# One encoder layer on one core: the MLP's up projection as seven products of halves, in turns with those of the down projection

## The chip, the cores and the metric

The kernel runs on one core of a Trainium2 chip. The metric is device time in microseconds (us) for one execution, weights read from HBM and outputs written back, everything between included. Less is better.

## What is computed

Two groups of 256 tokens share all weights, so the kernel treats them as T = 512 tokens of width D = 1024. In float32:

```
def encoder_layer(x, mem, ...):
    h = rms_norm(x, norm1_g)
    proj = h @ w_in                      # q, k, v of three attentions, three gates
    ... banded, dilated and memory attention ...
    merged = (sigmoid(ga) * (oa @ w_branch_a) + sigmoid(gb) * (ob @ w_branch_b)
              + sigmoid(gm) * (om @ w_branch_m))
    x = x + merged @ w_out
    h2 = rms_norm(x, norm2_g)
    x = x + jnp.square(jax.nn.relu(h2 @ w_up)) @ w_down    # w_up 1024 x 4096, w_down 4096 x 1024
    return x                             # then a final rms_norm
```

The change lies in the last three lines of the layer. The norm factor of h2 is not applied before the MLP: since the squared ReLU is homogeneous, the kernel multiplies the result of the down projection by the inverse mean square of each token (`rr`).

## The kernel before

**Three products for one.** Every float32 matrix is split into a rounded upper part (`hi`) and the remainder (`lo`), and `mm3` (line 193) makes one product as three TensorE matmuls: hi with hi, hi with lo, lo with hi. ScalarE (ACT) makes each hi by a copy, VectorE (DVE; in the attention stage GpSimd, POOL) makes each lo by a subtraction. A weight tile is 128 partitions by 1024 elements, 512 KB: one DMA, one ACT copy, one DVE subtraction.

**Units.** The program is a list of units, each a function and the weight tiles that it wants; `run()` calls them in order. Before the matmuls of a unit it fetches the tiles that are needed, behind them those of the next three needs (`ahead`): DMA, hi and lo stand that far ahead of their use. DVE, ACT and TensorE (PE) keep the order in which the program is written; the DMA queues of SyncE (SP) and POOL get theirs from a scheduler. Work on a finished product waits in a list, `later`, that is emptied (`flush`) behind the matmuls of the next unit. Subtractions for lo tiles wait in a list, `lows`, that `lower()` empties ahead of every unit.

**The stages.** Memory keys and values, the projections and attentions, the gates and branches, the output projection (`out_proj`, eight units of 24 matmuls, with h2 as eight tiles `h` of 128 features by 512 tokens), then the MLP.

**The MLP.** The 4096 inner features go in eight chunks `c` of 512. In chunk c, `up` makes four tiles of 128 features by 512 tokens, each in two halves of 12 matmuls of 512 columns; `put_up` takes ReLU and square on ACT into `UP`. The down projection of chunk c-1 stands between these halves, as seven products of halves instead of eight (Strassen's scheme in Winograd's form): `form` makes the sums of quarters of UP (DVE), their hi (ACT) and lo (DVE); `parts` makes the sums of quarters of the weights. One tile T holds a quarter, and becomes the next sum when POOL issues a DMA that adds another quarter onto it in place (`accum_op`), which has to wait for the lo tile that was made of it. `product` runs 12 matmuls of 512 columns, and `add_to` adds the two PSUM banks of a product to running sums (`acc`) on DVE. Chunk 7 is done without this (`last_down`): its weights and its four inner tiles (`LAST`) are used as they are, output quarter by output quarter.

Of the kernel before, what the change touches and what calls it, by code (L numbers as in the profile page):

```python
# [10 lines left out]
F32 = mybir.dt.float32  # L11
# [66 lines left out]
def encoder_kernel(ctx: ExitStack, tc: tile.TileContext, a: dict, out: bass.AP):  # L78
# [20 lines left out]
    def h2(s="h", dt=F32):  # L99
        return sb.tile([P, T], dt, tag="h2", name=nm(s), bufs=20)  # L100
# [10 lines left out]
    def f(x):  # L111
        return x.bitcast(F32)
# [57 lines left out]

    lows = []

    def lower(keep=0):
        for fn in lows[:len(lows) - keep]:
            fn()
        del lows[:len(lows) - keep]

    def run():
        need = [(i, s) for i, (_, srcs) in enumerate(units) for s in srcs]
        got, at = [[] for _ in units], 0  # L180
        done = 0
        for i, (fn, srcs) in enumerate(units):
            done += len(srcs)
            for fetch in (True, False):
                while at < min(len(need), done + (0 if fetch else ahead[0])):
                    u, s = need[at]
                    got[u].append(s[0]() if callable(s[0]) else chunk(*s))
                    at += 1
                if fetch:
                    lower()  # L190
                    fn(*got[i])

    def mm3(o, wh, wl, xh, xl, first, last, more=False):
# [565 lines left out]
        unit(flush)  # L759


    MG, wb, sg = [], [], {}

    def gate(w, ff, br):
# [40 lines left out]

    unit(lambda: merge(KD - 1))


    X1, H = [], []

    def out_proj(w):
        ff = len(H)
        r = h2("xr")
        A.dma_start(r, a["xT"][:, ff])
        p = bank()
        fm(w, M, p)
        V.tensor_tensor(r, p, r, op=ALU.add)
        X1.append(r)
        x = s4("h")
        A.activation(x[:, 0], r, AF.Copy, scale=gains[:, 2, ff:ff + 1])  # L820
        V.scalar_tensor_tensor(x[:, 1], r, gains[:, 2, ff:ff + 1], f(x[:, 0]), op0=ALU.mult,
                               op1=ALU.subtract)
        H.append(x)

    for ff in range(KD):
        unit(out_proj, (a["w_o"][ff],))

# [14 lines left out]
    def mlp_pool():  # L842
        stages.close()
        at[0] = stages.enter_context(tc.tile_pool(name="ml", bufs=1))

    def block_tile():
        return at[0].tile([P, 1024], F32, tag="blk", name=nm("blk"), bufs=8)

    def turn_x1(t, hh):

# [51 lines left out]
    def load_blocks(c):  # L902

        if c in blocks:
            return
        t = {n: block_tile() for n in "T2BC"}
        for n, b in (("T", "11"), ("2", "21"), ("C", "12"), ("B", "22")):
            SP.dma_start(t[n], block(c, b))
        G.dma_start(t["C"], block(c, "22"), accum_op=ALU.add)
        blocks[c] = t  # L910

    def parts(c, n):

        def go():
            load_blocks(c)
            hi, lo = w_tile(), w_tile()
            src = blocks[c][n[0]]
            A.activation(hi, src, AF.Copy)

            def low():  # L920
                V.tensor_tensor(lo, src, f(hi), op=ALU.subtract)
                if n[1:]:
                    G.dma_start(src, block(c, n[1:]), accum_op=ALU.add)  # L923

            lows.append(low)
            return hi, lo
        return go

# [2 lines left out]
    def form(c, name):  # L931

        lo, hi = UP[c, 0], UP[c, 1]
        A11, A21, A12, A22 = lo[:, :, :S], lo[:, :, S:], hi[:, :, :S], hi[:, :, S:]

        def less(u, v):
            d = h2("f").rearrange("p (j t) -> p j t", j=2)
            V.tensor_tensor(d, u, v, op=ALU.subtract)
            return d

        if name in ("P1", "P2", "Q4"):
            src = {"P1": A11, "P2": A12, "Q4": A22}[name]
        elif name == "Q5":
            src = forms[c, "S1"] = less(A21, A22)
        elif name == "Q6":
            src = forms[c, "S2"] = less(A11, forms.pop((c, "S1")))
        elif name == "P7":
            src = less(A11, A21)
        else:
            src = less(A12, forms.pop((c, "S2")))  # L950
        x = s4("f")
        xh, xl = (x[:, i].rearrange("p (j t) -> p j t", j=2) for i in range(2))
        A.activation(xh, src, AF.Copy)
        lows.append(lambda: V.tensor_tensor(xl, src, f(xh), op=ALU.subtract))
        forms[c, name] = x

    acc, banks = {}, {}

    def add_to(k, i, p, op=ALU.add):
        if (k, i) in acc:  # L960
            V.tensor_tensor(acc[k, i], acc[k, i], p, op=op)
        else:
# [1 line left out]
            A.activation(acc[k, i], p, AF.Copy, scale=1.0 if op == ALU.add else -1.0)  # L964


    PRODUCTS = dict(P1=("T12", "a", "V", -1), P2=("2", "a", "11", 1), Q5=("T22", "d", "G", 1),
                    Q6=("T21", "c", "V", 1), P7=("C", "e", "G", -1), Q3=("B", "d", "12", 1), Q4=("T", "e", "21", 1))

    def product(w, c, name):  # L970
        _, bk, to, sign = PRODUCTS[name]
# [86 lines left out]
    unit(mlp_pool)  # L1058
    ORDER = ("P1", "P2", "Q5", "Q6", "P7", "Q3", "Q4")


    SUMMED = {1: ("12", "12"), 2: ("11", "11"), 3: ("21", "21"), 4: ("12", "V"), 5: ("21", "V", 1), 6: ("22", "G")}

    def make(c, n):
        unit(lambda: form(c, ORDER[n]))

    for c in range(NC):
        for h in range(8):
            ff, half = 4 * c + h // 2, h % 2
            unit(lambda *w, ff=ff, half=half: up(w[0] if w else None, ff, half), *([(a["w_up"][ff],)] if half == 0 else []))  # L1070
            if c == 0:
                unit(lambda h=h: turn_x1(h % 4, h // 4))
            if h == 1 and c < NC - 1:
                unit(lambda c=c: load_blocks(c))
            if h == 7 and c == NC - 2:
                unit(fetch_x1)
            if c == NC - 1 and h == 6:
                unit(lambda: ahead.__setitem__(0, 2))
            if c == NC - 1 and h in SUMMED:
                unit(lambda n=SUMMED[h]: later.append(lambda: combine(*n)))  # L1080
            if c and h < 7:
                for n in ((1, 2) if h == 0 else (h + 2,)):
                    if n < 7:
                        make(c - 1, n)
                unit(lambda w, c=c - 1, n=ORDER[h]: product(w, c, n), (parts(c - 1, PRODUCTS[ORDER[h]][0]),))
        if c == 0:
            unit(inv_ms)
            unit(lambda: ahead.__setitem__(0, 3))
        if c < NC - 1:
            make(c, 0)  # L1090
    unit(lambda *w: (kept.update({(0, 0): w[0], (1, 0): w[1]}), last_down(0, (0, 1))),
         *[(block(NC - 1, n),) for n in ("11", "21")])
    unit(lambda: later.append(lambda: combine("22", "V")))
# [84 lines left out]
```

## Time and profile before

| | |
|---|---|
| median of 3 runs (lowest, highest) | 857.63 us (856.81, 858.55) |
| the profiled execution | 859.08 us |
| its span, from first to last instruction | 857.3 us |
| mean granted clock of PE | 0.993 |
| busy: PE, weight loads of PE, DVE, ACT, POOL | 844.4, 703.8, 462.8, 397.1, 216.0 us |

The profile is of one execution, 1.45 us above the median, with 1.8 us outside its span. A busy share is a mean over the whole span; what a change in one stage is worth has to be read in that stage. In the rows "ps" is a PSUM bank, "w" a hi or lo weight tile, "raw" and "blk" weight tiles as they come from HBM, "h" the tiles of h2, "f" a form, "u" inner features, "mg" the merged branches. Nearly every operation is recorded at L72, the line of a helper.

### The profile page before, as it was taken

The numbers are of one execution on the slowest core, as the hardware profiler recorded it, in microseconds if no ns is written. First come the engines' busy times: TensorE is split into PE (matmuls) and PEld (weight loads), VectorE is DVE, ScalarE is ACT, GpSimd is POOL, SyncE is SP. The second block draws the span as 40 slices with busy tenths as digits, with TensorE's granted clock in tenths as the row PEclk, the third lists the DMA queues.
The fourth block names the chain that finished last, engine by engine and source line by source line (L and its number), as shares of the span: only waits on it lengthen the run. The fifth ranks groups of instructions, "written<-read, shape, count | busy, mean of one in ns | idle before, by whom it ended". The sixth has DMA issues, their size and how long they took to land.

```text
span 857.3 us, 10785 instructions
## 1 busy us (share of the span) xinstructions
PE 844.4 (99%) x4080; PEld 703.8 (82%) x4080; DVE 462.8 (54%) x737; ACT 397.1 (46%) x690; POOL 216.0 (25%) x161
## 2 busy tenths in 40 slices
PE   9999999999999999999999999999999999999996
PEld 7788998888888888888888788888888888888885
DVE  6575535465452311423435542465767666767895
ACT  6455545565554333222323227564445353545453
POOL 2314554656556543211123000000000000000001
PEclk9999999999999999999999999999999999999998
DMA  8343122324241228432322445374747465645322
GB/s 284 115 119 109 62 99 86 98 63 115 85 119 64 75 74 286 132 99 86 110 99 74 147 147 161 110 204 107 205 109 208 111 185 121 178 120 172 75 75 98
DMA packets 47468, 106.87 MB, mean 125 GB/s; under 512 B 19358, under 2 KB 19604, under 8 KB 47416
## 3 DMA queue, kind: packets, MB, share of 16 engines
q1 hardware_dynamic: 39992, 85.69, 30.2%
q0 software_dynamic: 4256, 14.73, 9.7%
q10 hardware_dynamic: 3168, 5.77, 2.0%
q8 instruction: 32, 0.52, 0.3%
q14 instruction: 20, 0.16, 0.1%
HBM read 101.93 MB, written 4.24 MB: 124 GB/s over the span
## 4 chain that ended last, share of the span: by engine, by line
PE 84%; DVE 8%; ACT 5%; issue 2%; DMA 1%; POOL 0%; POOLq 0%; SPq 0%; DVEq 0%; ACTq 0%
PE ps L72 77%; PE sc L72 3%; PE o L72 2%; DVE w L72 2%; PE tp L72 2%; ACT w L72 2%; DVE f L72 1%; ACT sp L72 1%; DVE sp L72 1%; DMA mr<-in_memT 1%; ACT f L72 1%; DVE sq L72 0%; ACT r L72 0%; DVE mg L72 0%; DVE acc L72 0%
## 5 line engine op out<-in xcount | busy, mean ns | idle before, releaser
L72 PE MATMUL ps<-x,w 128*128 128x512 f32 x1080 | 252.5, 391 | 0.0
L72 PEld LDWEIGHTS ps<-x,w 128*128 128x128 f32 x1080 | 201.0, 188 | 41.3
L72 PE MATMUL ps<-h,w 128*128 128x512 f32 x768 | 184.5, 391 | 0.0
L72 PEld LDWEIGHTS ps<-h,w 128*128 128x128 f32 x768 | 143.7, 188 | 29.5
L72 PE MATMUL ps<-w,f 128*128 128x512 f32 (+1 forms) x696 | 164.1, 387 | 1.3 <-DVE acc L72 1.0
L72 DVE TENSOR_TENSOR w<-raw,w 128x1024 fp32r<-128x1024 f32 (+1 forms) x79 | 96.4, 1223 | 115.3 <-ACT w L72 115.2
L72 PEld LDWEIGHTS ps<-w,f 128*128 128x128 f32 x696 | 128.7, 188 | 29.9 <-issue 3.4
L72 ACT ACTIVATE w<-raw 128x1024 fp32r<-128x1024 f32 (+2 forms) x116 | 119.7, 1036 | 21.9 <-DMA raw<-in_w_mem 7.5
L161 POOL TENSOR_TENSOR w<-raw,w 128x1024 fp32r<-128x1024 f32 (+1 forms) x37 | 87.3, 2361 | 120.1 <-ACT w L72 94.9
L72 DVE TENSOR_TENSOR w<-blk,w 128x1024 fp32r<-128x1024 f32 x49 | 59.5, 1224 | 47.7 <-ACT w L72 47.6
L923 POOL DMA_DIRECT2D blk<-in_w_dn x21 | 18.1, 864 | 240.2 <-DVE w L72 240.2
L72 ACT ACTIVATE w<-blk 128x1024 fp32r<-128x1024 f32 x49 | 50.7, 1047 | 15.4 <-DMA blk<-in_w_dn 15.4
L72 DVE TENSOR_TENSOR acc<-acc,ps 128x512 f32<-128x512 f32 x82 | 52.9, 682 | 2.9 <-PE ps L72 2.9
L72 ACT ACTIVATE f<-f 128x512 fp32r<-128x512 f32 x28 | 17.7, 633 | 75.4 <-DVE f L72 75.4
L72 ACT ACTIVATE sp<-sp,st 128x256 f32<-128x256 f32 (+1 forms) x48 | 25.8, 538 | 57.7 <-DVE st L72 57.7
L72 ACT ACTIVATE g<-ps 128x512 f32<-128x512 f32 x16 | 9.6, 598 | 88.4 <-PE ps L72 88.4
L72 DVE TENSOR_TENSOR sum<-o,lo 64x256 f32<-64x256 f32 x24 | 10.0, 417 | 66.5 <-ACT lo L72 66.3
L72 PE MATMUL ps<-mg,w 128*128 128x512 f32 x192 | 44.2, 391 | 1.5 <-ACT mg L72 0.9
L72 PEld LDWEIGHTS ps<-mg,w 128*128 128x128 f32 x192 | 36.0, 188 | 9.6 <-ACT mg L72 1.3
L72 ACT ACTIVATE r<-ps 128x512 f32<-128x512 f32 x32 | 18.9, 591 | 50.7 <-PE ps L72 50.7
L72 PE MATMUL ps<-w,x 128*128 128x384 f32 (+1 forms) x192 | 39.9, 363 | 0.0
L469 POOL TENSOR_TENSOR sp<-sp,st 128x512 f32<-128x512 f32 (+1 forms) x32 | 36.7, 1147 | 6.5 <-DVE st L72 3.6
(146 smaller groups left out, 959.2 us busy)
## 6 DMA issues: line engine op xcount, KB each, us to landing
raw<-in_w_up SPq DMA_DIRECT2D x32, 512.0 KB, 4.7
blk<-in_w_dn SPq DMA_DIRECT2D x28, 512.0 KB, 6.7
blk<-in_w_dn POOLq DMA_DIRECT2D x28, 512.0 KB, 5.7
raw<-in_w_g SPq DMA_DIRECT2D x24, 512.0 KB, 3.3
raw<-in_w_b SPq DMA_DIRECT2D x12, 512.0 KB, 3.3
raw<-in_w_bam SPq DMA_DIRECT2D x8, 512.0 KB, 3.3
raw<-in_w_o SPq DMA_DIRECT2D x8, 512.0 KB, 3.2
raw<-in_w_mem SPq DMA_DIRECT2D x7, 512.0 KB, 3.3
```

Of the source, the lines that this page charges most:

```text
L72: return self.tc.keep_in_program_order(method(*args, **kw))
L161: sub[0].tensor_tensor(lo[:, c], raw[:, c], f(hi[:, c]), op=ALU.subtract)
L469: G.tensor_tensor(s[:, :, :w], s[:, :, :w], st[:, 6:8].unsqueeze(2).to_broadcast([P, 2, w]), op=ALU.mult)
L923: G.dma_start(src, block(c, n[1:]), accum_op=ALU.add)
```

## The change

1. **Up projection of chunks 1 to 7.** `seven` makes it of seven products. Rows of the result are halved by features (two tiles of 128 each), columns by group of tokens (256 each), the sum over 1024 by halves of 512. A product is 24 matmuls of 256 columns into one bank, 168 matmuls a chunk where there were 96 of 512 columns. Sums of quarters of the weights are made as in the down projection, with two tiles T and C and four accumulating DMAs a chunk; the quarters come from HBM in pieces of 2 KB. `take` puts the products together: three copies on ACT and five additions on DVE a chunk, and `put` takes ReLU and square.
2. **Sums of h2.** They are the same for all chunks, and `halves_of` makes them once, in eight steps, during chunk 0 (which keeps the plain `up`) and at the start of chunk 1. The last sum overwrites the second group's half of the first four h tiles.
3. **Turns.** One up product and one down product alternate, seven pairs a chunk. Both use the order P1, P2, Q5, Q3, Q6, P7, Q4, in which each sum held in T is used two pairs behind the one before; in the down projection Q6 stood right behind Q5. Quarters 21 and 22 are loaded by themselves into `raw` tiles rather than `blk` tiles.
4. **Lists.** `lower()` is gone. `tick()` stands at the head of `up`, of a product of either projection, and of `last_down` (there behind the flush). It runs what is in `wlows` (lo of weights, and the accumulating DMA that follows), in `lows` (lo of forms) and in `soon` (steps on ACT); what these add to the lists is run one tick later.
5. **Output projection.** The first two units are one: six eighths of the sum for both tiles first, then the last two eighths of each.
6. **Chunk 7.** Its inner tiles come by `put_last`, in pieces of 256 tokens.

```
+    def tick():
+        for todo in (wlows, lows, soon):
+            now = todo[:]
+            todo.clear()
+            for fn in now:
+                fn()
...
-                    lower()
...
+        def go(n, w):
+            tick()
...
+            for j in range(2):
+                for k in range(4):
...
+                    xh, xl = form_of(X, forms, n, k)
+                    mm3(b[:, j * S:(j + 1) * S], w[0][:, c], w[1][:, c], xh, xl, new and j == k == 0, k == 3, j > 0 or not new)
+            flush(9)
+            later.append(lambda: take(n, b))
...
-            lows.append(low)
+            wlows.append(low)
...
     def last_down(hh, ts, n0=0, n1=512, part=0):
         flush(9)
-        lower()
+        tick()
...
+    def put_last(i, h, r):
+        A.activation(r, r, AF.Square)
...
+        for j in range(2):
+            x, u, t = LAST[2 * h + j], r[:, j * S:(j + 1) * S], slice(i * S, (i + 1) * S)
+            A.activation(x[:, 0, t], u, AF.Copy)
+            lows.append(lambda x=x, u=u, t=t: V.tensor_tensor(x[:, 1, t], u, f(x[:, 0, t]), op=ALU.subtract))
```

The instructions move as follows at the three places of which the prediction speaks. On PE, at the start of the output projection before; mg711 and mg718 are the last two of the eight merged tiles, w698 and w699 hi and lo of the first weight tile:

```order
L72 MATMUL ps720_4077<-mg710_4021,w699_3969 128x512
L72 MATMUL ps720_4077<-mg711_4024,w698_3968 128x512 x2
L72 MATMUL ps720_4077<-mg711_4024,w699_3969 128x512
L72 MATMUL ps720_4077<-mg718_4072,w698_3968 128x512 x2
L72 MATMUL ps720_4077<-mg718_4072,w699_3969 128x512
L72 MATMUL ps726_4114<-mg705_4006,w703_4001 128x512 x2
```

and after, where the rows of the second weight tile (w703) with the first six merged tiles stand ahead of these:

```order
L72 MATMUL ps720_4080<-mg710_4021,w703_4001 128x512 x2
L72 MATMUL ps720_4080<-mg710_4021,w704_4002 128x512
L72 MATMUL ps719_4079<-mg711_4024,w698_3968 128x512 x2
L72 MATMUL ps719_4079<-mg711_4024,w699_3969 128x512
L72 MATMUL ps719_4079<-mg718_4072,w698_3968 128x512 x2
L72 MATMUL ps719_4079<-mg718_4072,w699_3969 128x512
```

The first use of mg718 was PE's 22nd matmul of the stage; it is now the 40th, behind 18 of each tile and three with mg711.

On DVE, after, one steady chunk has 44 instructions; these are those from the running sums of the first down product of a chunk (ps5962, ps5969) to those of the second:

```order
L72 TENSOR_TENSOR acc844_4744<-acc844_4744,ps1055_5962 128x512
L72 TENSOR_TENSOR acc845_4746<-acc845_4746,ps1056_5969 128x512
L72 TENSOR_TENSOR f1064_6018<-u1001_5628,f1053_5956 128x512
L72 TENSOR_TENSOR f1065_6020<-u1034_5811,f1064_6018 128x512
L72 TENSOR_TENSOR w1061_6011<-blk996_5603,w1060_6010 128x1024
L72 TENSOR_TENSOR w1070_6043<-raw1071_6044,w1069_6042 128x1024
L72 TENSOR_TENSOR f1066_6022<-f1065_6020,f1066_6022 128x512
L72 TENSOR_TENSOR acc863_4824<-acc863_4824,ps1055_5962 128x512
L72 TENSOR_TENSOR acc864_4826<-acc864_4826,ps1056_5969 128x512
```

Each pair of products has two lo tiles of weights of its own there (w1061 of the down projection, w1070 of the up projection); before, a chunk had 11 of them, now it has 14.

On DVE in `last_down`, before: ps1242 and ps1243 are the sums of the first two token tiles, f1241 the last lo tile of LAST, ps1252 the sum of the third token tile:

```order
L72 TENSOR_TENSOR f1241_6823<-u1230_6756,f1241_6823 128x512
L72 TENSOR_TENSOR w1246_6854<-raw1244_6852,w1245_6853 128x1024
L72 TENSOR_TENSOR w1249_6860<-raw1247_6858,w1248_6859 128x1024
L72 SCALAR_TENSOR_TENSOR blk1178_6488<-ps1242_6826,rr_92,blk1178_6488 128x512
L72 SCALAR_TENSOR_TENSOR blk1179_6490<-ps1243_6827,rr_92,blk1179_6490 128x512
L72 TENSOR_TENSOR blk1178_6488<-blk1178_6488,gf1182_6496 128x512
L72 SCALAR_TENSOR_TENSOR blk1180_6492<-acc827_4664,rr_92,blk1180_6492 128x512
L72 SCALAR_TENSOR_TENSOR blk1181_6494<-acc828_4666,rr_92,blk1181_6494 128x512
L72 SCALAR_TENSOR_TENSOR blk1180_6492<-ps1252_6873,rr_92,blk1180_6492 128x512
```

and after, with ps1313 and ps1314 for the first two token tiles and f1269, f1270 for the lo parts that the third one (ps1323) reads:

```order
L72 TENSOR_TENSOR w1320_7619<-raw1318_7617,w1319_7618 128x1024
L72 SCALAR_TENSOR_TENSOR blk1246_7148<-ps1313_7585,rr_92,blk1246_7148 128x512
L72 SCALAR_TENSOR_TENSOR blk1247_7150<-ps1314_7586,rr_92,blk1247_7150 128x512
L72 TENSOR_TENSOR blk1246_7148<-blk1246_7148,gf1250_7156 128x512
L72 SCALAR_TENSOR_TENSOR blk1248_7152<-acc844_4744,rr_92,blk1248_7152 128x512
L72 SCALAR_TENSOR_TENSOR blk1249_7154<-acc845_4746,rr_92,blk1249_7154 128x512
L72 TENSOR_TENSOR f1269_7276<-e1297_7454,f1269_7276 128x256
L72 TENSOR_TENSOR f1270_7277<-e1297_7454,f1270_7277 128x256
L72 SCALAR_TENSOR_TENSOR blk1248_7152<-ps1323_7634,rr_92,blk1248_7152 128x512
```

The lo parts stood ahead of the two scalings of the first sums; they now stand behind these, a multiplication by the final gain and two more scalings.

More of the change, by code (lines that the diff above doesn't have):

```diff
@@ L759, in encoder_kernel, with late_pool, block_tile, halves_of @@
         unit(flush)
+    def late_pool():
+        stages.close()
+        at[0] = stages.enter_context(tc.tile_pool(name="ml", bufs=1))
+    def block_tile():
+        return at[0].tile([P, 1024], F32, tag="blk", name=nm("blk"), bufs=8)
+    SEVEN = ("P1", "P2", "Q5", "Q3", "Q6", "P7", "Q4")
+    ONTO = dict(P1="12", Q5="22", Q6="21")
+    BANK = dict(P1="a", P2="a", Q5="d", Q3="d", Q6="c", P7="e", Q4="e")
+    def halves_of(X, forms):
+        u, l = slice(0, S), slice(S, 2 * S)
+        kept = {}
+        def pair():
+            return h2("d").rearrange("p (j t) -> p j t", j=2)
+        def parted(d, hi, lo):
+            def upper():
+                A.activation(hi, d, AF.Copy)
+                lows.append(lambda: V.tensor_tensor(lo, d, f(hi), op=ALU.subtract))
+            soon.append(upper)
+        def put(S, j, d):
+            hi, lo = (x[:, 512 * j:512 * j + 512].rearrange("p (j t) -> p j t", j=2) for x in forms[S])
+            parted(d, hi, lo)
+        def less(x, y, out):
+            e = pair()
+            V.tensor_tensor(e, f(x), f(y), op=ALU.subtract)
+            V.tensor_tensor(out, e[:, 0], e[:, 1], op=ALU.add)
+        def minus(x, d, out):
+            V.tensor_tensor(out, f(x[:, 0]), d, op=ALU.subtract)
+            V.tensor_tensor(out, out, f(x[:, 1]), op=ALU.add)
+        def s1(j):
+            d = kept[1, j] = pair()
+            for i in range(2):
+                k = 2 * j + i
+                less(X[k][:, :, l], X[k + 4][:, :, l], d[:, i])
+            put("Q5", j, d)
+        def s2(j):
+            d = kept[2, j] = pair()
+            for i in range(2):
+                minus(X[2 * j + i][:, :, u], kept[1, j][:, i], d[:, i])
+            put("Q6", j, d)
+        def s4_(j):
+            d = pair()
+            for i in range(2):
+                minus(X[2 * j + i + 4][:, :, u], kept[2, j][:, i], d[:, i])
+            put("Q3", j, d)
+        def s3(j):
+            for i in range(2):
+                x, d = X[2 * j + i], pair()[:, 0]
+                less(x[:, :, u], x[:, :, l], d)
+                parted(d, x[:, 0, l], x[:, 1, l])
+        return [lambda fn=fn, j=j: fn(j) for fn in (s1, s2, s4_, s3) for j in range(2)]
@@ L1020, in last_down @@
         flush(9)
-        lower()
+        tick()
         ps_ = {t: bank()[:, :n1 - n0] for t in ts}
@@ L1056, in scale_out @@
             (A, SP)[hh].dma_start(out[t * P:(t + 1) * P, hh * 512:(hh + 1) * 512], xt[t][:, hh])
-    unit(mlp_pool)
-    ORDER = ("P1", "P2", "Q5", "Q6", "P7", "Q3", "Q4")
-    SUMMED = {1: ("12", "12"), 2: ("11", "11"), 3: ("21", "21"), 4: ("12", "V"), 5: ("21", "V", 1), 6: ("22", "G")}
-    def make(c, n):
-        unit(lambda: form(c, ORDER[n]))
-    for c in range(NC):
[L1068 to L1073, printed above, removed]
+    HF, u7 = {}, {}
@@ new lines, in start_up, with up_seven, block, put @@
+    def start_up():
+        for n in ("Q5", "Q6", "Q3"):
+            HF[n] = [sb.tile([P, 1024], F32R, tag="s4", name=nm("f"), bufs=21) for _ in range(2)]
+    def up_seven(c):
+        def block(n):
+            k, f0 = int(n[0]) - 1, 4 * c + 2 * (int(n[1]) - 1)
+            return a["w_up"][f0:f0 + 2, :, k * 512:(k + 1) * 512].rearrange("f p c -> p f c")
+        def put(n, x):
+            i, h = int(n[0]) - 1, int(n[1]) - 1
+            if (c, h) not in UP and c < NC - 1:
+                UP[c, h] = sb.tile([P, 2, T], F32, tag="s4", name=nm("u"), bufs=21)
+            r = h2("r") if n == "11" else x
+            A.activation(r, x, AF.Relu)
+            if c == NC - 1:
+                return put_last(i, h, r)
+            A.activation(UP[c, h][:, :, i * S:(i + 1) * S], r.rearrange("p (j t) -> p j t", j=2), AF.Square)
+        return seven(H, HF, block, lambda: (block_tile(), block_tile()), put)
@@ new lines, in make, with down_unit @@
+    def make(c, n):
+        unit(lambda: form(c, SEVEN[n]))
+    def down_unit(c, n):
+        for m in ((1, 2) if n == 0 else (n + 2,)):
+            if m < 7:
+                make(c, m)
+        unit(lambda w: product(w, c, SEVEN[n]), (parts(c, PRODUCTS[SEVEN[n]][0]),))
+    pieces_up = halves_of(H, HF)
+    for h in range(8):
+        ff, half = h // 2, h % 2
+        unit(lambda *w, ff=ff, half=half: up(w[0] if w else None, ff, half), *([(a["w_up"][ff],)] if half == 0 else []))
+        unit(lambda h=h: turn_x1(h % 4, h // 4))
+        if h == 0:
+            unit(start_up)
+        if h < 6:
+            unit(pieces_up[h])
+        if h == 1:
+            unit(lambda: load_blocks(0))
+            u7[1] = up_seven(1)
+            unit(u7[1][0])
@@ L1074, in encoder_kernel @@
+    for c in range(NC):
+        for n in range(7 if c else 0):
+            unit(*u7[c][1][n])
+            if c == 1 and n in (1, 2):
+                unit(pieces_up[5 + n])
+            if n == 1 and c < NC - 1:
                 unit(lambda c=c: load_blocks(c))
-            if h == 7 and c == NC - 2:
-                unit(fetch_x1)
-            if c == NC - 1 and h == 6:
+            if n == 3 and c < NC - 1:
+                u7[c + 1] = up_seven(c + 1)
+                unit(u7[c + 1][0])
+            if c == NC - 1 and n == 6:
@@ L1078, in encoder_kernel @@
                 unit(lambda: ahead.__setitem__(0, 2))
[L1079 to L1085, printed above, removed]
+            if c == NC - 1 and n in SUMMED:
+                unit(lambda n=SUMMED[n]: later.append(lambda: combine(*n)))
@@ L1090, in encoder_kernel @@
             make(c, 0)
+        if c == NC - 2:
+            unit(fetch_x1)
+    unit(lambda: later.append(lambda: combine(*SUMMED[7])))
     unit(lambda *w: (kept.update({(0, 0): w[0], (1, 0): w[1]}), last_down(0, (0, 1))),
```

143 lines of the change are left out of this document (108 added, 35 removed).

## The prediction

> **What bounds the kernel now.** I read the page's busy times first, then the chain of work that ended last, then the table of stretches, and the waits of single instructions last. Two lines of the page, the first with busy time per engine, the second with the chain's shares:
>
> ```profile
> PE 844.4 (99%) x4080; PEld 703.8 (82%) x4080; DVE 462.8 (54%) x737; ACT 397.1 (46%) x690; POOL 216.0 (25%) x161
> ...
> PE 84%; DVE 8%; ACT 5%; issue 2%; DMA 1%; POOL 0%; POOLq 0%; SPq 0%; DVEq 0%; ACTq 0%
> ```
>
> PE is busy in 99% of the span, so only fewer or cheaper matmuls, or one of its few waits, can shorten the run. The chain in order of time (start, length, what) shows how regular the MLP is:
>
> ```profile
> 320.99 140.13 PE ps L72 x618
> ...
> 587.98 0.61 DVE acc L72
> 588.73 32.94 PE ps L72 x144
> ...
> 629.98 32.90 PE ps L72 x144
> ...
> 788.86 1.23 DVE w L72
> 790.09 1.22 DVE f L72 x2
> ...
> 794.17 0.61 DVE acc L72
> 794.91 51.94 PE ps L72 x228
> ```
>
> The first row gives the pitch of matmuls of 512 columns: 140.13 / 618 = 0.227 us. From 588.73 to 794.91 lie five chunks, 41.24 us each. A chunk has 96 matmuls of up and 84 of down; 180 x 0.227 = 40.8, so PE waits 0.4 us per chunk, for the running sum on DVE. The rest is matmuls end to end. The other engines and the DMA engines, from the table of stretches (busy time and instructions per engine, granted clock, DMA share, GB/s):
>
> ```profile
> 39.90:46.60 6.70, 6.70 (x23) 5.83 (x23) 3.79 (x6) 0.00 (x0) 4.90 (x8) 0.50 0.24 85
> 474.70:482.00 7.30, 7.30 (x32) 6.06 (x33) 3.36 (x4) 2.09 (x3) 0.00 (x0) 1.00 0.56 190
> 588.73:794.91 206.18, 205.33 (x900) 168.66 (x901) 142.29 (x181) 96.69 (x130) 16.39 (x20) 1.00 0.58 151
> 650.00:662.00 12.00, 12.00 (x54) 9.95 (x53) 10.65 (x14) 4.60 (x6) 1.73 (x2) 1.00 0.92 241
> 846.50:849.00 2.50, 2.50 (x22) 2.46 (x21) 1.96 (x5) 1.34 (x3) 0.34 (x2) 1.00 0.54 202
> ```
>
> In the five chunks DVE is busy 142.29 of 206.18 us, ACT 96.69, the DMA engines 58%. That is the room the change spends.
>
> **Up projection: matmuls.** It takes away 96 matmuls of 512 columns per chunk and puts 168 of 256 in. What one of those costs shows twice. The last 24 matmuls of the kernel are of 256 columns, and the stretch 846.50 to 849.00 lies inside them: 21 weight loads in 2.50 us, 0.119 each, at clock 1.00. And in the attention stage (chain again; sc are six matmuls of 256 columns, tp transposes of 128):
>
> ```profile
> 78.88 0.71 PE sc L72 x6
> ...
> 251.91 0.66 PE tp L72 x6
> ```
>
> 0.71 / 6 = 0.118. So two of 256 cost 0.24 against 0.227 for one of 512: seven eighths of the multiplications cost 0.93 of the time. I take 0.120, since the stretch has cut matmuls at its edges. A chunk becomes 168 x 0.120 + 84 x 0.227 = 20.2 + 19.0 = 39.2 us, 2.04 less than 41.24 (the 0.4 us wait is included as gone, because the order of units at a chunk's start is another). Seven chunks: **-14.3 us**. With 0.118 it is -16.6.
>
> **Can the others deliver?** DVE: 44 instructions per chunk, 14 lo tiles of weights (11 before) and 30 of 512 columns (7 lo and 4 sums of forms, 14 running sums, 5 of the up products). From start to start they take 1.23 and 0.61 us (rows at 788.86, 790.09, 794.17): 17.2 + 18.3 = 35.5 of 39.2 us, 91%. ACT's two kinds by their groups (after the bar: busy us, mean ns):
>
> ```profile
> L72 ACT ACTIVATE w<-blk 128x1024 fp32r<-128x1024 f32 x49 | 50.7, 1047 | 15.4 <-DMA blk<-in_w_dn 15.4
> ...
> L72 ACT ACTIVATE f<-f 128x512 fp32r<-128x512 f32 x28 | 17.7, 633 | 75.4 <-DVE f L72 75.4
> ```
>
> 14 x 1.05 + 18 x 0.63 = 26.0 of 39.2 us. That DVE at 91% does not hold PE up rests on slack: a weight's lo is made about three units (8.4 us) ahead of its use, one unit behind its hi. Going down the order of DVE with these lengths and letting each step wait for its product or its hi, I find DVE idle for about 3 us per chunk, and each lo 3 us or more early. So in the steady chunks I book nothing. The first chunk of this kind has more: the last sums of h on DVE (eight of 256 columns and four of 512), ten running sums as ACT copies, and the second weight tile of the down projection is fetched only as the chunk begins. One or two lo tiles should then be late by about one ACT copy: **+1.0 us**, between 0 and 2. Chunk 0 keeps its matmuls (96 x 0.227 and 32 transposes of 0.110, 25.3 us); the sums made beside it are 30 steps of at most 0.61, 18 us of a DVE that has only three lo tiles to make there; nothing booked.
>
> **Weight sums by DMA.** The rows for the five chunks by queue (packets, MB, share of 16 engines), the landing of the accumulating DMAs, and POOL's time for issuing one:
>
> ```profile
> q1 hardware_dynamic: 5760, 20.97, 30.1%
> q0 software_dynamic: 2736, 9.96, 27.4%
> ```
>
> ```profile
> DMA to landing us min/median/max: 5.2/5.5/8.9
> ```
>
> ```profile
> L923 POOL DMA_DIRECT2D blk<-in_w_dn x21 | 18.1, 864 | 240.2 <-DVE w L72 240.2
> ```
>
> A plain tile of 0.524 MB takes 0.301 x 206.18 / 40 = 1.55 us of all 16 engines, an accumulated one 0.274 x 206.18 / 19 = 2.97. A chunk had 8 and 4, and has 8 and 8: 36.2 us of 39.2, a share of 0.92 where it was 0.58. This counts stretched packets twice, but it is the share of the stretch 650 to 662, and a landing of 8.9 us will be common rather than the longest. A link of T's chain is hi 1.05, lo 1.23, issue 0.86, landing, and about 1.5 (my estimate) of standing in line: 10.1 us with 5.5, 13.5 with 8.9. The next hi is due four units (11.2 us) later. The excess falls on ACT, which has 13 us per chunk to spare, and inside the prefetch. Nothing booked; it is a rival below. POOL's own load is 8 x 0.86 = 7 us, nearer 14 if pieces of 2 KB double it.
>
> **Output projection.** PE's timeline around the last merged tile (start, length, count, idle before):
>
> ```profile
> 467.75 4.92 PE L72 MATMUL ps<-mg,w 128*128 128x512 f32 x21
> 473.56 0.49 PE L72 MATMUL ps<-mg,w 128*128 128x512 f32 x1 [0.89 <-ACT mg L72]
> 474.64 0.73 PE L72 MATMUL ps<-mg,w 128*128 128x512 f32 x2 [0.58 <-DVE mg L72]
> ```
>
> After 22 matmuls PE should be at 467.75 + 22 x 0.227 = 472.7; it is there at 474.64. With 39 matmuls ahead of mg718 it gets there at 476.6, after both its parts exist. **-1.9 us**; the lo of the second weight tile stands on DVE ahead of the lo of the merged tiles. Bounds: 0 to 2 of gain.
>
> **The tail.** Here the change adds a wait. `tick()` in `last_down` comes behind the flush, so the lo parts that the third token tile reads stand on DVE behind five steps, of which the first two wait for PE's own products. DVE's timeline of before:
>
> ```profile
> 830.25 0.69 DVE L72 TENSOR_TENSOR f<-u,f 128x512 fp32r<-128x512 f32 x1
> 830.84 2.48 DVE L72 TENSOR_TENSOR w<-raw,w 128x1024 fp32r<-128x1024 f32 x2
> 833.24 1.40 DVE L72 SCALAR_TENSOR_TENSOR blk<-ps,rr,blk 128x512 f32<-128x512 f32 x2
> 834.77 0.69 DVE L72 TENSOR_TENSOR blk<-blk,gf 128x512 f32<-128x512 f32 x1
> 835.38 1.41 DVE L72 SCALAR_TENSOR_TENSOR blk<-acc,rr,blk 128x512 f32<-128x512 f32 x2
> 836.71 0.75 DVE L72 SCALAR_TENSOR_TENSOR blk<-ps,rr,blk 128x512 f32<-128x512 f32 x1
> ```
>
> The lo that was done at 830.94 would now start at 836.71 and end about 837.0 (half of 0.61). PE wants it for its third matmul behind the second sum; that sum is whole three matmuls after the first (833.2), at 833.9, and the third matmul behind it would start near 834.1. Queued behind it on PE are all 82 matmuls left, so the run waits: **+2.9 us**. Bounds: 2 (if that DVE line runs earlier) and 6.3, for a long wait can also cost clock. In these rows of the chain PE stands aside from 32.0 to 39.6, and the stretch behind it has clock 0.50 for 6.7 us:
>
> ```profile
> 6.94 25.07 PE ps L72 x114
> ...
> 39.56 33.14 PE ps L72 x136
> ```
>
> That would lose 3.4 us; behind the 1.9 us at 473 the clock was 1.00. 2.9 is nearer to 1.9, so I book no clock loss. (The Trainium skill, "TensorE: Matmul & The Clock Gate", Part 1, puts the point at an idle window of about 3.4 us; no run here shows a wait of that size.)
>
> **Sum.** -14.3 + 1.0 - 1.9 + 2.9 = -12.3 us. The profiled execution, 859.08, would come to 846.8; from the median, 857.63, **845.3 us**.
>
> **Rivals.** *DVE paces the chunks.* For it: 91% with waits between DVE, ACT and PE in every unit; DVE's line has no spare buffer of time but 3.7 us per chunk, and a hi that waits for its DMA stops ACT and then DVE. Against it: no lo is wanted sooner than 3 us after it can be made. If its waits reach 4.7 us per chunk, a chunk takes 40.2: six steady chunks lose 1.0 each and the first 1.3 more, 845.3 + 7.3 = 852.6 us. Chance 0.18.
>
> *T's chain paces the chunks, and the kernel is slower.* Between the first and the last of the four uses of T lie 12 units, 33.6 us, and the prefetch adds at most 8.4: 42.0 less the last hi and lo (2.3) is 39.7, 13.2 for each of three links, which is a landing of 8.6 us. Each us beyond costs 3 per chunk, 21 in all; the gain of 12.3 is gone from 9.2 on. At 9.5 us: 845.3 + 7 x 2.7 = 864.2. For it: a share of 0.92 with two chains at once, and 8.9 seen. Against it: that was the longest, beside four plain loads, and the median was 5.5. Chance 0.12.
>
> *Weight loads show.* Were a load not covered by the matmul ahead, each of the 168 would cost 0.120 and up to 0.110 (the pitch of the transposes above, where 128 columns cover least) against 0.227 for 512: 38.6 us for the up part where it was 21.8, +117 us over seven chunks, about 970. That is a rule of the Trainium skill ("TensorE: Matmul & The Clock Gate", Part 3, The mechanism): loads overlap matmuls in flight only when they address other row groups. Here every load addresses all rows, and 0.119 with 21 loads in 2.50 us leaves no room for it: chance 0.01.
>
> **Numbers.** Forecast 0.67, DVE 0.18, T's chain 0.12, loads 0.01, and 0.02 that the tail and small waits take everything. 842 holds most of the cheaper pitch; 854 takes in the DVE case; slower ones stay outside. A difference of 0.2% (1.7 us) is about what can be told from none. Faster 0.84, same 0.03, slower 0.13.
>
> **What would show it.** Right: seven chunks of about 39.2 us between the first up matmuls of neighbours, 24 matmuls of 256 columns in 2.9 us, DVE near 90% and the DMA share near 0.9 there, no wait on mg at 473, one PE wait of 3 us for a lo (f) some 23 us before the end. Wrong: PE waits for w or f inside steady chunks (DVE), for which ACT waits on blk with landings over 9 us (T's chain), a pitch of 256 columns above 0.125, or no wait in the tail.

## The result, and the profile after

The changed kernel takes 872.66 us (median of 4, 869.08 to 874.92); the kernel before took 858.09 us beside it (median of 4, 856.81 to 858.80). The ratio is 1.0171, 95% interval 1.0146 to 1.0195: slower, where 845.3 us was forecast. The profiled execution took 872.51 us, with a span of 870.7 us.

From the page of the changed kernel, the busy time of each engine and the chain's shares:

```profile
PE 841.0 (97%) x4584; PEld 721.1 (83%) x4584; DVE 526.0 (60%) x839; ACT 434.3 (50%) x746; POOL 250.0 (29%) x189
...
PE 56%; DVE 15%; DMA 14%; issue 8%; ACT 6%; POOL 1%; SPq 0%; POOLq 0%; ACTq 0%; DVEq 0%
```

PE had 84% of the chain and has 56%; DMA had 1% and has 14%. Where in the run that is, PE's timeline tells (start, length, what, count, idle before). These are the first matmuls of chunk 1, the waits in chunk 1, in a steady chunk and in the tail:

```profile
537.19 3.11 PE L72 MATMUL ps<-h,w 128*128 128x256 f32 x24
...
558.12 4.42 PE L72 MATMUL ps<-f,w 128*128 128x256 f32 x24 [3.77 <-ACT e L72]
...
645.58 3.01 PE L72 MATMUL ps<-w,f 128*128 128x512 f32 x12 [1.45 <-DVE acc L72]
...
844.43 7.91 PE L72 MATMUL ps<-w,f 128*128 128x512 f32 x23 [4.09 <-DVE f L72]
```

Laid out by the starts of PE's matmuls in the two profiled executions (us; a chunk runs from its first up matmul to the next chunk's, chunk 7 to the first matmul of `last_down`; before, the values of chunks 1 and 7 are the mean of both):

| stretch | before | forecast | after |
|---|---|---|---|
| to the first matmul of chunk 1 | 538.77 | 536.9 | 537.19 |
| chunk 1 | 41.3 | 40.2 | 45.02 |
| chunks 2 to 6 | 206.2 | 196.0 | 209.26 |
| chunk 7 | 41.3 | 39.2 | 42.81 |
| behind it, to the last matmul | 21.8 | 24.7 | 28.58 |

The rows add up: 862.87 - 849.43 = 13.4 us, and the two times differ by 872.51 - 859.08 = 13.4. Against the forecast 13.3 us are lost in the five steady chunks, 4.8 in the first, 3.6 in the last, 3.9 in the tail. The output projection gave 1.7 of the 1.9 us booked: from its first matmul to that of chunk 1 it is 71.02 us before and 69.36 after, and the wait on mg is gone:

```profile
467.83 18.44 PE L72 MATMUL ps<-mg,w 128*128 128x512 f32 x79
```

In a steady chunk the chain shows what PE waits for in the end (start, length, what):

```profile
617.68 6.43 DMA blk<-in_w_up
624.68 0.72 POOL blk L859
625.39 9.90 DMA blk<-in_w_dn
635.32 1.06 ACT w L72
637.41 0.63 ACT u L72
638.04 0.96 ACT w L72
639.07 0.92 issue
640.17 0.69 DVE f L72
640.85 1.20 DVE acc L72 x2
...
644.84 0.69 DVE acc L72
645.58 1.67 PE ps L72 x6
```

The load of a block of C at 617.68 ends, POOL issues the accumulating DMA that stands next (L859), then the one of L1085, which lands 9.9 us later; ACT can then make a hi. POOL's timeline shows the line that these stand in:

```profile
616.73 0.86 POOL L1067 DMA_DIRECT2D blk<-in_w_dn  x1 [9.04 <-DVE acc L72]
619.68 1.21 POOL L873 DMA_DIRECT2D blk<-in_w_up  x1 [2.09 <-DVE w L72]
624.67 1.21 POOL L859 DMA_DIRECT2D blk<-in_w_up  x1 [3.79 <-DMA blk<-in_w_up]
625.39 1.42 POOL L1085 DMA_DIRECT2D blk<-in_w_dn  x1
```

and ACT's, the hi of the down projection's second sum in T (for Q5):

```profile
635.32 1.06 ACT L72 ACTIVATE w<-blk 128x1024 fp32r<-128x1024 f32 x1 [6.61 <-DMA blk<-in_w_dn]
```

L1067 is the sum C of the down projection, L873 the first link of the up projection's T, L859 the sum C of the next up chunk, L1085 the first link of the down projection's T. Chunk 3 starts at 624.1, and its third down product, which reads this hi and the lo behind it, is due some 14 us later; the hi is ready at 636.4. ACT works in order: its parts and copies for the next products stand behind the hi, then DVE's sums, then PE. The lo that L1085 had to wait for, that of the down projection's first tile T, was ready at 621.8 by DVE's timeline, so the link stood 3.6 us behind the other issues before its own:

```profile
620.55 1.23 DVE L72 TENSOR_TENSOR w<-blk,w 128x1024 fp32r<-128x1024 f32 x1
```

### The profile page after: what moved, and what is told of

Its sections match the earlier page's. It is cut to its first block, busy times and chain, and to the rows that moved or that the text cites. A ratio compares the mean times of both kernels' runs of the same rounds, so it can differ in the third digit from the quotient of the medians.

```text
span 870.7 us, 12038 instructions
## 1 busy us (share of the span) xinstructions
PE 841.0 (97%) x4584; PEld 721.1 (83%) x4584; DVE 526.0 (60%) x839; ACT 434.3 (50%) x746; POOL 250.0 (29%) x189
## 4 chain that ended last, share of the span: by engine, by line
PE 56%; DVE 15%; DMA 14%; issue 8%; ACT 6%; POOL 1%; SPq 0%; POOLq 0%; ACTq 0%; DVEq 0%
PE ps L72 49%; DMA blk<-in_w_dn 6%; DMA blk<-in_w_up 5%; DVE w L72 4%; ACT w L72 3%; PE sc L72 3%; PE o L72 2%; DVE acc L72 2%; DVE f L72 2%; PE tp L72 2%; DVE blk L72 2%; DMA mr<-in_memT 1%; DVE e L72 1%; DMA raw<-in_w_mem 1%; DVE d L72 1%
## 5 line engine op out<-in xcount | busy, mean ns | idle before, releaser
L72 PE MATMUL ps<-w,f 128*128 128x512 f32 (+1 forms) x696 | 168.4, 393 | 12.9 <-DVE acc L72 8.9
L72 PEld LDWEIGHTS ps<-w,f 128*128 128x128 f32 x696 | 127.9, 191 | 39.2 <-DVE acc L72 10.1
L72 PE MATMUL ps<-h,w 128*128 128x256 f32 (+1 forms) x768 | 109.5, 298 | 1.2 <-DVE e L72 1.2
L72 PEld LDWEIGHTS ps<-h,w 128*128 128x128 f32 x768 | 101.2, 191 | 8.3 <-issue 3.1
L72 DVE TENSOR_TENSOR w<-blk,w 128x1024 fp32r<-128x1024 f32 x70 | 85.5, 1222 | 35.9 <-ACT w L72 35.7
L72 ACT ACTIVATE w<-blk 128x1024 fp32r<-128x1024 f32 x70 | 72.2, 1051 | 47.3 <-DMA blk<-in_w_dn 43.0
L873 POOL DMA_DIRECT2D blk<-in_w_up x21 | 25.4, 1207 | 166.4 <-DVE w L72 160.0
L72 PEld LDWEIGHTS ps<-f,w 128*128 128x128 f32 x504 | 64.0, 195 | 9.2 <-ACT e L72 8.0
L72 PE MATMUL ps<-f,w 128*128 128x256 f32 x504 | 65.6, 287 | 5.6 <-ACT e L72 5.6
L1085 POOL DMA_DIRECT2D blk<-in_w_dn x21 | 21.5, 1023 | 63.4 <-DMA blk<-in_w_up 38.9
```

The costliest lines, as they stand in the source:

```text
L72: return self.tc.keep_in_program_order(method(*args, **kw))
L873: G.dma_start(by2(src), block(ONTO[n]), accum_op=ALU.add)
```

## The experiments

**First theory:** the sums come late because C of the up chunk waits for its own load at the head of POOL's queue, and PE waits because the second product of a pair shares a bank with the first and has to wait until that is read. **Rivals:** VectorE paces the chunks; the DMA engines are full; operands are late in any case.

**C of the up chunk later.** POOL's MLP transfers keep program order (`GO`), and that sum is written behind the first pair of products of its own chunk, not with its load in the chunk before:

```
+        def sum_c():
+            GO.dma_start(by2(t["C"]), block("22"), accum_op=ALU.add)
...
+            if n == 1:
+                unit(u7[c][1])
```

> The changed kernel with another order of the accumulating DMAs on GpSimd's queue: the sum C of the next up chunk, which waits for its own plain load, goes behind the first link of the down projection's T instead of ahead of it, and the MLP's issues on GpSimd stand in the order in which the program is written. Nothing is left out. Theory (head of the line: T's first link is issued only when C's load has landed, and its sum then waits behind C's): ScalarE's wait of 6.6 us for T at Q5 of the down projection shrinks to 2 us or less, a chunk falls to 39.5-40.3 us, and the run is 8 to 14 us shorter than the changed kernel. Rival (the DMA engines' share itself, at 0.86 to 0.91, makes the sums late in any order): the wait moves to another sum, the chunk stays at 41-42 us.

858.99 us (10 runs), 1.0015 of the kernel before (1.0005 to 1.0026), 13.7 below the changed kernel. Chunks 2 to 6 take 39.34 us each. The table of stretches over four of them (busy time and count of PE, PEld, DVE, ACT, POOL; clock; DMA share; GB/s):

```profile
600.00:757.00 157.00, 157.00 (x1007) 143.26 (x1007) 138.02 (x177) 96.05 (x129) 33.78 (x32) 1.00 0.92 215
```

PE has no wait left, with all eight sums, DVE busy 138.02 of 157 (88%) and the DMA engines 92%. So neither VectorE nor the DMA engines' total paced the chunks; the share of 0.92 and the 39.2 us of the forecast were right. On POOL the link (617.24) now stands behind one sum (614.85) instead of three; C of the up chunk follows it (617.82), and so does C of the down chunk, issued at 626.83:

```profile
614.85 1.20 POOL L72 DMA_DIRECT2D blk<-in_w_up  x1 [11.71 <-DVE w L72]
617.24 0.91 POOL L72 DMA_DIRECT2D blk<-in_w_dn  x1 [1.20 <-DVE w L72]
617.82 1.57 POOL L72 DMA_DIRECT2D blk<-in_w_up  x1
```

**No sums.** All `accum_op` transfers of the MLP left out:

```
-            G.dma_start(by2(t["C"]), block("22"), accum_op=ALU.add)
-                    G.dma_start(by2(src), block(ONTO[n]), accum_op=ALU.add)
...
```

> The changed kernel without the accumulating DMAs of the MLP: the sums of weight blocks C and T of both projections are left out, so those products use the blocks as first loaded; every matmul, copy and subtraction stays. Theory (the sums on GpSimd's queue land late, ScalarE waits for them in its own order and the copies and sums of the turns wait behind it): a steady chunk falls from 41.9 to 39.2-39.6 us, the wait in the first seven-product chunk falls below 1.5 us, and the run is near 845-850. Rival 1 (VectorE paces the chunks): the chunk stays at 41.5-42 us, the run within 3 us of the changed kernel plus whatever the first chunk gives. Rival 2 (the up projection's 256-wide matmuls cost more than was read from the rows): the chunk stays over 41 us with no waits on TensorE.

857.56 us (10 runs; ratio 1.0005, 0.9995 to 1.0015). Chunks 2 to 6 take 39.34 us, with a DMA share of 0.32. The theory of late sums holds, VectorE as the pacer falls. But chunk 1 keeps its wait of 4.15 us and its 45.0 us, chunk 7 its 42.8, and the run misses 845 to 850: what is lost outside the steady chunks has other causes.

**Own banks.** `new = True` in both `go` and `product`, which leaves out the accumulation of the second product of a pair onto the first.

> The changed kernel with every one of the seven products starting in a PSUM bank of its own: the accumulation of the second product of a pair onto the first in the bank is left out, the number of matmuls, copies and sums stays. Theory (ScalarE's lateness reaches TensorE because the second product of a pair waits until the first one's bank has been read, one unit later): TensorE's waits for a sum or a copy in the middle of a chunk go, the chunk falls to 39.2-40 us. Rival (ScalarE and VectorE are late for the operands as well): the waits only move to operands' hi and lo parts and the chunk stays over 41 us.

868.45 us (1.012, 1.0092 to 1.0148). Chunks 2 to 6 take 40.9 to 44.2 us, 210.1 together: here the theory falls. PE's timeline in one:

```profile
633.78 0.50 PE L72 MATMUL ps<-w,f 128*128 128x512 f32 x1 [1.24 <-ACT w L72]
635.04 2.79 PE L72 MATMUL ps<-w,f 128*128 128x512 f32 x11 [0.76 <-DVE w L72]
```

PE waits for the weight itself, hi and then lo; with shared banks it waited, by the chain above, for sums that were late by the same wait of ACT. In chunk 1 it is different: 40.14 us where the changed kernel has 45.02. There the shared bank is what holds PE. Chunk 7 falls as well, to 40.21 us, but the tail takes 32.35, with a wait of 6.69 us for a lo of VectorE where the changed kernel has 4.09: what is gained there is lost behind it.

**One sum fewer, twice.** Either line alone taken out of the changed kernel, the first of the up projection, the second of the down projection:

```
-            G.dma_start(by2(t["C"]), block("22"), accum_op=ALU.add)
```
```
-        G.dma_start(t["C"], block(c, "22"), accum_op=ALU.add)
```

> The changed kernel without one of its eight accumulating DMAs per chunk: the sum C of the up projection's chunk is left out (its product uses the block as first loaded). The order of the other seven on GpSimd's queue stays. Theory (that sum stands ahead of the first link of the down projection's T and waits for its own plain load): the chunk falls to 39.3-39.6 us, as without any sum, and the run is 12 to 16 us shorter than the changed kernel. Rival (eight sums are too many for the DMA engines or for the queue, whichever stands where): one sum fewer gives about an eighth of what all eight gave, 0.3 us per chunk; the chunk stays over 41 us.

> The counterpart: the changed kernel without the sum C of the down projection's chunk, again one of eight accumulating DMAs and again with the order of the others kept. The up projection's C still stands ahead of T's first link. Theory: the chunk stays at 41.2-42 us and the run within 4 us of the changed kernel. Rival (any sum fewer helps by its share of the DMA engines): the same gain as without the up projection's C.

857.49 us (8 runs; 0.9997, 0.9987 to 1.0008) and 857.35 us (8 runs; 1.0000, 0.9988 to 1.0013). Both have chunks of 39.34 us. The first was expected; the second contradicts the theory, and the rival of an eighth falls with both. Without the down projection's C the up projection's C still stands ahead of the link, and waits 0.7 us for its load where it waited 3.8 (the load itself lands after 3.3 us, and after 6.4 in the changed kernel, where the sum C of the down projection is under way); ACT's wait:

```profile
625.27 1.06 ACT L72 ACTIVATE w<-blk 128x1024 fp32r<-128x1024 f32 x1 [1.08 <-DMA blk<-in_w_dn]
```

Two readings are left: the number of sums ahead of the link, or the wait for a load among them.

**Three ahead, none waiting.** All eight sums in program order, both sums C issued between the two first links, for blocks that have long been loaded:

```
+            if n == 6 and 0 < c < NC - 2:
+                unit(lambda c=c: load_blocks(c + 1))
...
+            if n == 6 and 0 < c < NC - 1:
+                unit(u7[c + 1][1])
```

> All eight sums, in program order on GpSimd: first link of the up projection's T, the sums C of both projections, then the first link of the down projection's T. So three sums stand ahead of that link as in the changed kernel, but the plain loads that the two sums C need have landed long before, so nothing on the queue waits for a load. Two readings of the runs so far. By the number of sums ahead (each 3.5 us, one after another): the link lands some 30 us into the chunk and TensorE still waits 0.5 to 1.5 us per chunk, chunk 40 to 41 us. By the wait for a plain load at the head of the line (5 us between two issues in the changed kernel): the chunk is 39.34 us and the run near 859.

875.17 us (2 runs; 1.0199, 1.0170 to 1.0229), chunks 3 to 6 of 43.2 to 43.4 us. POOL's and ACT's timelines:

```profile
615.54 1.20 POOL L72 DMA_DIRECT2D blk<-in_w_up  x1 [11.99 <-DVE w L72]
616.26 1.42 POOL L72 DMA_DIRECT2D blk<-in_w_dn  x1
616.82 2.10 POOL L72 DMA_DIRECT2D blk<-in_w_up  x1
617.94 1.92 POOL L72 DMA_DIRECT2D blk<-in_w_dn  x1
```

```profile
633.01 1.06 ACT L72 ACTIVATE w<-blk 128x1024 fp32r<-128x1024 f32 x1 [8.44 <-DMA blk<-in_w_dn]
```

No issue waits for a load, and yet the link lands 15.0 us after its issue (the two rows of DMA issues at 616.8 and 617.9: KB each, us to landing):

```profile
blk<-in_w_up POOLq DMA_DIRECT2D x1, 512.0 KB, 13.0
blk<-in_w_dn POOLq DMA_DIRECT2D x1, 512.0 KB, 15.0
```

So three sums ahead of the link are enough to make it late, without any wait for a load, and by more than either reading expected. What the wait for the load adds by itself in the changed kernel is not separated by a run. The variants side by side, from the issue of the first link of the up projection's T to the landing of the down projection's:

| kernel | sums ahead of the link | that time, us | steady chunk, us |
|---|---|---|---|
| C later | 1 | 8.3 | 39.34 |
| no C of up | 2 | 9.7 | 39.34 |
| no C of down | 2 | 11.2 | 39.34 |
| changed kernel | 3 | 15.6 | 41.9 |
| three ahead | 3 | 17.4 | 43.3 |

Up to 11.2 us costs nothing, from there to 15.6 it begins to cost, and 1.8 us more costs 1.4 us a chunk.

**The tail.** In the changed kernel VectorE's timeline ahead of PE's wait, which ends at 844.43, has two weight lo tiles, four scalings and a multiplication by the gain in front of the two lo parts that PE waits for:

```profile
838.21 2.36 DVE L72 TENSOR_TENSOR w<-raw,w 128x1024 fp32r<-128x1024 f32 x2
...
843.96 0.75 DVE L72 TENSOR_TENSOR f<-e,f 128x256 fp32r<-128x256 f32 x2
```

The two lines at the head of `last_down` exchanged:

```
-        flush(9)
         tick()
+        flush(9)
```

> The changed kernel with one edit: at the start of the last down chunk the queued sums of the turns come before the queued lo parts, not behind them. Shown after the change: PE waits 4.5 us at 840 us for a lo part that VectorE makes last, behind two weight lo parts and two sums, and some ten matmuls behind that wait take 427 ns each. Theory (the wait is only the order of VectorE's queue): the wait shrinks below 1.5 us, the half-speed matmuls go with it, and the run is 5 to 7 us shorter than the changed kernel, near 866. Rival (ScalarE's hi of that form is late in itself): the wait stays over 3 us and the time within 1.5 us of the changed kernel's. Neither expects a steady chunk of other than 41.9 us.

866.88 us (1.0113, 1.0095 to 1.0130), 5.8 below the changed kernel. From the end of chunk 7 to the last matmul it takes 22.7 us where it was 28.58; the steady chunks, which the edit does not touch, took 42.5 us in its profiled execution. PE's row at that place, for the one of 844.43 above:

```profile
842.43 16.31 PE L72 MATMUL ps<-w,f 128*128 128x512 f32 x82 [0.62 <-DVE f L72]
```

The 82 matmuls behind it take 16.31 us, 0.2 each. In the changed kernel the stretch behind the wait shows the clock (columns as above):

```profile
845.10:849.20 4.10, 4.10 (x11) 3.23 (x10) 0.10 (x1) 0.00 (x0) 0.00 (x0) 0.50 0.00 0
```

**The first chunk.** C later and the tail's exchange, and the last two pieces of the sums of h2 made in chunk 0, not behind the second and third product of chunk 1:

```
-        if h < 6:
-            unit(pieces_up[h])
+        unit(pieces_up[h])
...
-            if c == 1 and n in (1, 2):
-                unit(pieces_up[5 + n])
```

> Nothing left out. The order of the sums as in the run with C later, the two queue calls swapped in the last down chunk, and the last two pieces of S3 made in chunk 0 instead of between the second and third product of the first seven-product chunk. Theory (three separate delays that add up): steady chunks 39.34 us, no wait of 4.15 us in the first chunk, no wait of 4.5 us in the tail; 859.0 less 5.8 less 3.5 to 4.2 gives 849 to 850, faster than the kernel before by about 0.9%. Rival for the first chunk (ScalarE and VectorE are behind by then in any order): a wait of over 2 us stays there, and the run is near 853.

848.10 us (4 runs), 0.9880 of the kernel before (0.9863 to 0.9897): 24.6 us below the changed kernel, and faster than both. Chunk 1 takes 41.15 us instead of 45.0, steady chunks 39.34. In the changed kernel ACT's timeline had these rows there, the second of them the copy of the third product:

```profile
556.64 0.42 ACT L72 ACTIVATE h<-d 128x256 fp32r<-128x256 f32 x1 [0.65 <-DVE d L72]
...
557.49 0.58 ACT L72 ACTIVATE e<-ps 128x512 f32<-128x512 f32 x1
```

A wait is left in chunk 1, for a lo of the first form, which VectorE makes behind the two pieces:

```profile
541.74 2.56 PE L72 MATMUL ps<-w,f 128*128 128x512 f32 x10 [1.45 <-DVE f L72]
```

Two other places for the pieces, in chunk 1 behind the fourth and fifth product and behind the second and fourth (`n in (3, 4)`, `n in (1, 3)`):

> As the kernel with all three edits, but the last two pieces of S3 stay in the first seven-product chunk and are made after its fourth and fifth product (they were made after the second and third; its sixth product reads them). Theory (what held TensorE in that chunk was that ScalarE's parts of S3 stand ahead of its copy of the third product, which the fourth product's matmuls wait for): neither the wait of 4.15 us nor the one of 1.85 us that came when chunk 0 made the pieces, the run 1 to 2 us shorter than the kernel with three edits, 846.5. Rival (VectorE is behind in that chunk whatever the order): 2 us or more are waited there at some other place.

> As the kernel with all three edits, but the last two pieces of S3 are made after the second and fourth product of the first seven-product chunk, so that only the later one has moved, from the tick that copies the third product to the next one. Theory: the copy of the third product is no longer behind a part of S3, the wait of 4.15 us falls below 1 us. Rival (the first piece sets VectorE back as well): 1 to 3 us stay.

851.94 us (5 runs; 0.9930, 0.9918 to 0.9943) and 848.76 us (4 runs; 0.9894, 0.9876 to 0.9912). The first missed: the wait for the third product's copy is gone, but a new one as long stands two products later, because the piece is made right ahead of the product that reads it:

```profile
568.02 3.10 PE L72 MATMUL ps<-h,w 128*128 128x256 f32 x17 [3.67 <-DVE h L72]
```

The second did as its theory said, with chunk 1 at 41.42 us and two waits left:

```profile
553.41 3.13 PE L72 MATMUL ps<-f,w 128*128 128x256 f32 x24 [0.57 <-ACT e L72]
...
571.40 2.87 PE L72 MATMUL ps<-h,w 128*128 128x256 f32 x22 [0.87 <-DVE e L72]
```

**The last chunk.** The kernel with the three edits, without the `combine` calls of chunk 7 and the tail:

```
-            if c == NC - 1 and n in SUMMED:
-                unit(lambda n=SUMMED[n]: later.append(lambda: combine(*n)))
...
```

> As the kernel with all three edits, but the sums that add the running sums of the down projection to the output rows in the last chunk and the tail are left out (12 instructions of VectorE). Theory (VectorE has no idle time in the last chunk): TensorE's waits of 1.9 and 1.6 us there vanish and the run is 3 to 4 us shorter than the kernel with the three edits, 844 to 845. Rival (those waits come from the order of ScalarE and VectorE, not from VectorE's load): at least one of them stays over 1 us.

845.53 us (2 runs; 0.9854, 0.9834 to 0.9874), 2.6 below, where 3 to 4 were expected; seven pairs of sums are left out, 14 instructions and not 12. Chunk 7 takes 41.08 us for 42.84. The two waits with the three edits:

```profile
796.06 3.02 PE L72 MATMUL ps<-w,f 128*128 128x512 f32 x12 [1.61 <-DVE acc L72]
...
811.50 3.10 PE L72 MATMUL ps<-h,w 128*128 128x256 f32 x24 [1.18 <-DVE e L72]
```

Without these sums the first shrinks and the second stays, so the expectation holds for one of the two:

```profile
793.14 3.01 PE L72 MATMUL ps<-w,f 128*128 128x512 f32 x12 [0.29 <-DVE acc L72]
...
808.34 3.11 PE L72 MATMUL ps<-h,w 128*128 128x256 f32 x24 [0.95 <-DVE e L72]
```

So these sums make half of what chunk 7 loses against a steady chunk. In the other half Q4 of the up projection waits until VectorE has read P7's bank, and that subtraction still stands in line: even without the sums VectorE is idle for only 0.14 us between 797.6 and 810.5. What else fills VectorE in chunk 7 alone was not tried.

**The same sums on GpSimd.** Four of the seven pairs as a scaling and an addition on POOL:

```
+                GO.tensor_scalar(z, x, rr[:, t, less:less + 1], None, op0=ALU.mult)
+                GO.tensor_tensor(y, y, z, op=ALU.add)
```

> As the kernel with all three edits, and four of the pairs of sums that add a down product of the last chunk to the output rows go from VectorE to GpSimd, as a scaling and an addition each (16 instructions on GpSimd for 8 on VectorE). Theory (in the last chunk VectorE has no idle time left, and TensorE waits 1.9 and 1.6 us there for its running sums): those waits fall below 0.8 us each, and the run is 2 to 3.5 us shorter than the kernel with the three edits. Rival (GpSimd is slower at it and shares data paths with VectorE, or its sums delay the accumulating DMAs queued behind them): the waits stay or grow and the time is the same or longer.

855.35 us (9 runs; 0.9969, 0.9958 to 0.9980), 7.3 above the kernel with three edits: the rival's outcome. From POOL's timeline, and PE's wait for the running sums:

```profile
791.53 3.59 POOL L72 TENSOR_SCALAR z<-acc,rr 128x512 f32<-128x512 f32 x1
795.21 1.28 POOL L72 TENSOR_TENSOR blk<-blk,z 128x512 f32<-128x512 f32 x1
```

```profile
795.45 4.60 PE L72 MATMUL ps<-w,f 128*128 128x512 f32 x12 [2.83 <-DVE acc L72]
```

The eight pairs of these take 2.8 to 5.4 us each on POOL for one DVE instruction of 0.7. PE waits 2.83 and 4.87 us in chunk 7, and chunk 7 takes 50.63 us. VectorE is not relieved either: beside POOL's sums its three `f<-f,f` sums take 1.09 to 1.79 us each, where they take 0.68 without them, while its running sums, which read PSUM, stay at 0.68. The row of one:

```profile
786.71 1.79 DVE L72 TENSOR_TENSOR f<-f,f 128x512 fp32r<-128x512 f32 x1
```

How much of the loss comes from this and how much from POOL's own times is not separated.

## Why the prediction was wrong

**Up matmuls, -14.3 us: right.** Undelayed chunks take 39.34 us, forecast 39.2; five of them gain 9.5 us.

**"About 1.5 (my estimate) of standing in line" for a link of T, "nothing booked": the step that failed.** It priced a link by its own landing and never asked in which order POOL's queue would hold the sums. Around the start of a chunk three sums stand ahead of the down projection's first link. The four land one after another, 4.0 to 4.7 us apart. From its lo the link needed 13.5 us to land, 3.6 in line and 9.9 from issue to landing, where the term gave 7.9 (0.86 + 5.5 + 1.5). "The excess falls on ACT, which has 13 us per chunk to spare" failed with it: ACT waited 6.61 us for this one tile, and the copies that PE needed stood behind. That cost 12.6 us over five chunks, 209.26 against 5 x 39.34; C later, which moves the sums and leaves none out, brings all of it back. The rival "T's chain paces the chunks, and the kernel is slower" named the place; its price, 2.7 us a chunk with all three links late, was nearly met by one link alone, 2.5. It counted seven chunks, and five show it; its 864.2 us is still 8.5 short of the measured time, and the terms below make the rest. "For which ACT waits on blk with landings over 9 us" was the sign to look for, and it is there: 6.61 us, 9.90 us.

**"DVE idle for about 3 us per chunk, and each lo 3 us or more early": right for steady chunks, wrong for the ends.** With C later the steady chunks run at 88% of DVE without a wait. Chunk 1 was booked at +1.0 and lost 5.8, a wait of 3.8 and 24 matmuls in 4.42 us that otherwise take 3.04: ACT's parts of the last sum of h2 stand ahead of its copy of the third product, whose bank the fourth needs. Own banks (40.14 us) and moving the pieces (41.15 and 41.42) show it. Chunk 7 was not considered apart from the others, though VectorE adds the output sums there; it lost 3.6, and half of that is shown to be these sums.

**The tail, +2.9 between 2 and 6.3: sized too small.** It cost 6.8. The wait was 4.1 us, as the lo stands behind VectorE's sums and two weight lo tiles, and it did cost clock: some ten matmuls at 427 ns where 227 is the pitch, about 2 us more, in the stretch at 0.50. I had put the clock loss outside the sum because 2.9 is nearer to 1.9. (The Trainium skill, "TensorE: Matmul & The Clock Gate", Part 1, has the clock fall after an idle window of about 3.4 us; this wait agrees.)

**Output projection, -1.9: right**, 1.7 measured.

With three of the four delays taken out the kernel runs at 848.10 us, 2.8 above the forecast: in its profiled execution chunk 1 is 1.0 longer than forecast, the steady chunks together 0.7, chunk 7 3.6, and the tail 2.0 shorter.

## What to carry to other kernels

Where several transfers share a queue that works in order, cost a transfer by what stands ahead of it at that moment, not by its own landing: a queue that keeps up over a whole turn can still hold three in a row ahead of the one that is wanted. Look at the first and the last turn of a loop by themselves, since they carry extra steps on the engines that only just keep up. In these runs every wait of TensorE in the MLP that was 2.8 us or longer cost twice, once as a wait and once in the clock; none of 1.6 us or less did by itself.

## What the hardware showed that was not expected

In seven places of the changed kernel PE's matmuls start 1.57 to 1.89 us apart, and the clock stays at 1.00 behind them. In the kernel with sums on GpSimd a gap of 3.11 us from start to start, 2.83 of it idle by the row, cost the clock: eight matmuls of 422 to 427 ns stand behind it. With own banks two waits with one matmul between them were enough, and the clock is 0.51 in the 3.5 us behind:

```profile
718.20 0.50 PE L72 MATMUL ps<-w,f 128*128 128x512 f32 x1 [1.92 <-ACT w L72]
719.46 4.38 PE L72 MATMUL ps<-w,f 128*128 128x512 f32 x11 [0.76 <-DVE w L72]
```

So a wait shorter than the 3.4 us that the Trainium skill, "TensorE: Matmul & The Clock Gate", Part 1, gives as the window can be enough.

Accumulating DMAs of one queue land one after another: with three ahead the four issued within 2.4 us from 615.54 on land 5.9, 7.9, 13.0 and 15.0 us after their issues, at 621.4, 624.2, 629.8 and 633.0. The first lands about as early as one alone (5.3 to 5.9 us). Their issue takes POOL 0.86 to 0.91 us for rows of 4 KB and 1.20 for pieces of 2 KB, and 1.4 to 2.1 where several follow at once.
